# A decoder trunk on one core: other places for the staging of spilled expert activations and for the recurrent layer's modulation rows, and softplus on GpSimd

## The chip, the cores and the metric

The kernel runs on one core of one Trainium2 chip. The metric is the device time of one execution in microseconds. Engines are named as in the profile: PE is TensorE (matmuls), PEld its weight loads, DVE is VectorE, ACT is ScalarE, POOL is GpSimd, SP is SyncE, which here only issues DMA transfers. Each engine has a queue of instructions that it works off in order; an instruction that has to wait holds up all that stand behind it in its queue.

## The reference

The model has two layers. Layer 0 mixes over time with a gated linear recurrence (RG-LRU), layer 1 with multi-head latent attention; in both a PEER layer of 128 x 128 experts follows. Sequence 512, width 1024, all in fp32. Cut to what this change touches:

```python
mod = (silu(c) @ ada_w[l] + ada_b[l])             # six rows of 1024 for each layer
sh1, sc1, g1, sh2, sc2, g2 = split(mod, 6)
h = rmsnorm(x, norm_mix_g[l]) * (1 + sc1) + sh1
gate_in, rec_in = split(h @ w_in, 2)
gate = gelu(gate_in)
xc = causal convolution of rec_in, 4 taps
r, i = sigmoid(xc @ wa + ba), sigmoid(xc @ wx + bx)      # four blocks of 256
log_a = -8 * r * softplus(-lam)
a, b = exp(log_a), sqrt(-expm1(2 * log_a)) * (i * xc)
y = (gate * linear_scan(a, b)) @ w_out
x = x + g1 * y
h = rmsnorm(x, norm_ffn_g[l]) * (1 + sc2) + sh2
x = x + g2 * peer(h)
```

`peer` takes for each token and head the 16 best pairs of two lists of 128 keys, and adds up `g * gelu(h . u[e]) * v[e]` over the experts `e` chosen.

## The kernel before

**Layout and arithmetic.** Activations lie transposed, [128 features, 512 tokens], eight such blocks for the width. A matmul in fp32 is made of three in a shorter format (`mm3`, lines 187 to 189): each operand is split in a high part, a copy on ACT (line 162), and a low part, the difference, mostly on DVE (line 163). A weight tile of 512 KB (128x1024) is loaded by SP into a ring of four buffers `raw`, and split into `whi` and `wlo`, of which there are three each.

**Modulation rows.** `ada(n)` makes 128 of the values of `mod`: SP loads 512 KB (`ada_raw`, line 147), and one DVE instruction multiplies them by silu(c) and sums (line 151) into a column of `mod`. There are 112 of them. `adas(n)` takes the next n from the list `todo`. Layer 0's first norm uses the first 16, the residual of the recurrent layer columns 16 to 23, the norm behind it 24 to 39.

**The recurrent layer.** Norm and the recurrent half of the input projection (`rec`), the convolution (line 385, three DVE steps for each of eight blocks), eight gate blocks (`gate`, line 391, each one weight tile `w_in` and 24 matmuls), the block matrices (`ri`, line 403), the decay (lines 408 to 417), the scan, the product with the gate, its split (`yh`, `yl`), the output projection (`wo`), the residual (line 282) and the sum of squares of the next norm (`nacc`, line 226), which `st` (line 232) sums over the partitions. `softplus_neg` (lines 285 to 328) works on a tile of 128x8 with some fifty short instructions; the decay reads its results `sp_s2` and `sp_s4`. 24 modulation rows are issued in two groups of 12, the first after the convolution's last step, the second after the fourth product with the gate (`held`), through two buffers of the pool `late`.

**PEER.** Three of the four blocks of 128 tokens are done densely: for each of 128 expert groups t, the product with `u` (`u_part`), gelu, multiplication by the routing weights (`weigh`), and the product with `v` (`v_part`), which adds up in PSUM over all t. The fourth block's experts are gathered row by row (`gather_steps`): 256 gathers on GpSimd's queue for each layer, each with one DVE step (lines 1131 and 1136). The routing weights are made in groups and written to DRAM (`wscr`). While that goes on, the products with `u` of the first 93 groups are done already (`LEAD`). Of these, 8 stay in the space of `x`, 9 in a ring of 12 buffers `gact`, and the next 76 (`SPILL`) are written to DRAM (`gscr`) from a staging tile `gsp` with three buffers (lines 908 to 910). `gsp` belongs to the pool `dec`, which closes at line 994. The pool `vp` opens next, and gets the same space: it has `wt` (the routing weights of eight groups, 1.5 MB, line 1007), and the split products `ah` and `al`. `wfirst` (line 1003) has the weights of the first two groups in another pool. In the loop over t, `gact` is loaded back from `gscr` nine groups ahead of its use. The list `wts` shares the gathers that are left over the groups (`goal`).

**What sets the order.** The program is written in a tile framework that orders the instructions of each engine by a simulated time line; `issue_after(i)` keeps an instruction behind another one. Buffers are waited for by semaphores, and a tile in a space that another pool has used waits for all that used it there.

## Time and profile before

| what | value |
|---|---|
| runs | 3152.28, 3153.51, 3155.0 us; median 3153.51 |
| the profiled execution's own time | 3153.72 us |
| its span (the page's first line) | 3151.9 us |
| granted TensorE clock over the span | 0.977 |
| PE, DVE, ACT, POOL busy | 95%, 82%, 44%, 27% |
| DMA | 821 MB, mean 261 GB/s |

The stages follow each other in time: the recurrent layer to about 213 us; layer 0's routing with the products with `u` to 812; its accumulation over the groups to 1515; attention to 1840; layer 1's PEER layer to about 3110, with the start of its accumulation at about 2440. In the rows of the profile a wait stands as "engine tile line <- engine or DMA that ended it: total us, count, longest". In a time line a row has start, length, engine, line, operation, tiles and, in brackets, the idle time before it with what ended it.

### The profile page before, as it was taken

Reading aid. Unit: us, or ns where it says so; the run is one execution under the profiler, and the core shown is the slowest. Engines: PE = TensorE matmul, PEld = TensorE weight load, DVE = VectorE, ACT = ScalarE, POOL = GpSimd, SP = SyncE. Lnnn points to the kernel's source line nnn. Section 1 sums busy time; section 2 is a strip of 40 time slices with the busy share of each in tenths; the row PEclk is TensorE's granted clock in tenths of the full one; section 3 lists DMA queues with packets and bytes.
Section 4 is the critical chain, followed back from the end, with each engine's and each line's share of the span. In section 5 each row is a group of like instructions: output and inputs, shape, how many; then the busy total and the mean of one; then the engine's idle time right before and its main releaser. Section 6 shows DMA issues by size and latency. Waiting matters only on the chain.

```text
span 3151.9 us, 43413 instructions
## 1 busy us (share of the span) xinstructions
PE 2996.1 (95%) x15462; PEld 2651.3 (84%) x15462; DVE 2571.8 (82%) x4895; ACT 1387.8 (44%) x1974; POOL 854.5 (27%) x653
## 2 busy tenths in 40 slices
PE   7989999999899999999899989999999899999997
PEld 6569999999777889998677679999999788889996
DVE  8879999897788878888668768999886777778886
ACT  5643255555233333333466542355554333333333
POOL 0000004342123214444256500014432311134440
PEclk9989999999999999999899999999999999999999
DMA  6644568998989999999213244469998999999994
GB/s 248 202 139 145 175 222 305 313 338 317 325 303 365 347 353 323 336 342 317 71 47 107 76 142 137 138 224 330 321 337 303 353 320 306 322 314 344 338 331 141
DMA packets 345112, 821.15 MB, mean 261 GB/s; under 512 B 33600, under 2 KB 179136, under 8 KB 338496
## 3 DMA queue, kind: packets, MB, share of 16 engines
q1 hardware_dynamic: 239632, 460.91, 43.9%
q0 software_dynamic: 73728, 268.47, 24.2%
q10 hardware_dynamic: 31536, 89.00, 7.4%
q8 instruction: 122, 2.00, 0.3%
q14 instruction: 94, 0.77, 0.1%
HBM read 730.98 MB, written 87.29 MB: 260 GB/s over the span
## 4 chain that ended last, share of the span: by engine, by line
PE 55%; DVE 6%; DMA 2%; ACT 2%; issue 2%; POOL 1%; DVEq 0%; SPq 0%; POOLq 0%; ACTq 0%
PE acc L188 8%; PE acc L187 8%; PE acc L189 8%; PE u L187 7%; PE u L189 7%; PE u L188 7%; PE wps L857 3%; DMA vraw<-in_v_dram 1%; PE pq L187 1%; PE pq L188 1%; PE pq L189 1%; ACT p L667 1%; DVE vl L163 1%; DVE ada_junk L151 1%; DVE p L662 1%
## 5 line engine op out<-in xcount | busy, mean ns | idle before, releaser
L1127 POOL DMA_INDIRECT grow<-in_u_dram,idx x256 | 345.0, 1348 | 1371.2 <-DVE oh L804 706.0
L187 PE MATMUL u<-hh,wlo 128*128 128x384 f32 x2048 | 690.8, 337 | 3.0 <-ACT gsp L909 3.0
L189 PE MATMUL u<-hh,whi 128*128 128x384 f32 x2048 | 688.5, 336 | 0.0
L188 PE MATMUL u<-hl,whi 128*128 128x384 f32 x2048 | 687.1, 335 | 0.0
L187 PE MATMUL acc<-vh,al 128*128 128x512 f32 x1536 | 570.3, 393 | 40.2 <-DVE al L163 30.6
L188 PE MATMUL acc<-vl,ah 128*128 128x512 f32 x1536 | 603.1, 393 | 0.0
L189 PE MATMUL acc<-vh,ah 128*128 128x512 f32 x1536 | 603.0, 393 | 0.0
L1127 POOL DMA_INDIRECT grow<-in_v_dram,idx x256 | 350.1, 1368 | 685.0 <-DVE gacc L1136 383.1
L163 DVE TENSOR_TENSOR wlo<-raw,whi 128x1024 fp32r<-128x1024 f32 x315 | 383.3, 1218 | 113.2 <-ACT whi L162 111.5
L163 DVE TENSOR_TENSOR vl<-vraw,vh 128x1024 fp32r<-128x1024 f32 x256 | 313.2, 1224 | 163.9 <-ACT vh L162 158.9
L162 ACT ACTIVATE whi<-raw 128x1024 fp32r<-128x1024 f32 (+2 forms) x372 | 358.3, 964 | 143.4 <-PE acc L189 30.4
L187 PEld LDWEIGHTS u<-hh,wlo 128*128 128x128 f32 x2048 | 386.5, 189 | 6.5 <-ACT gsp L909 3.7
L188 PEld LDWEIGHTS u<-hl,whi 128*128 128x128 f32 x2048 | 385.9, 188 | 2.7
L189 PEld LDWEIGHTS u<-hh,whi 128*128 128x128 f32 x2048 | 385.7, 188 | 0.0
L187 PEld LDWEIGHTS acc<-vh,al 128*128 128x128 f32 x1536 | 290.8, 190 | 104.2 <-issue 21.1
L189 PEld LDWEIGHTS acc<-vh,ah 128*128 128x128 f32 x1536 | 290.6, 189 | 61.4
L188 PEld LDWEIGHTS acc<-vl,ah 128*128 128x128 f32 x1536 | 291.1, 190 | 59.6 <-DVE vl L163 0.3
L1136 DVE SCALAR_TENSOR_TENSOR gacc<-grow,gdot,gacc 128x1024 f32<-128x1024 f32 x254 | 324.9, 1279 | 17.2 <-DMA grow<-in_v_dram,idx 16.0
L162 ACT ACTIVATE vh<-vraw 128x1024 fp32r<-128x1024 f32 x256 | 268.4, 1050 | 156.4 <-DMA vraw<-in_v_dram 54.1
L162 ACT ACTIVATE ah<-gact 128x384 fp32r<-128x384 f32 x240 | 125.8, 524 | 460.6 <-PE acc L189 257.9
L1131 DVE CUSTOM_DVE_ANT_0 grow<-grow,hn 128x1024 f32<-128x1024 f32 x256 | 309.3, 1219 | 9.2 <-DMA grow<-in_u_dram,idx 8.9
L860 ACT ACTIVATE stg<-wps 128x512 f32<-128x512 f32 x192 | 187.3, 1108 | 54.7 <-PE wps L857 46.2
(345 smaller groups left out, 4193.6 us busy)
## 6 DMA issues: line engine op xcount, KB each, us to landing
raw<-in_uT_dram SPq DMA_DIRECT2D x256, 512.0 KB
vraw<-in_v_dram SPq DMA_DIRECT2D x256, 512.0 KB
ada_raw<-in_adaw_dram SPq DMA_DIRECT2D x112, 512.0 KB
wscr<-stg ACTq DMA_DIRECT2D x48, 1024.0 KB
wt<-wscr SPq DMA_DIRECT2D x32, 1536.0 KB
gscr<-gsp ACTq DMA_DIRECT2D x152, 192.0 KB
gact<-gscr SPq DMA_DIRECT2D x152, 192.0 KB
raw<-in_w_pq_dram SPq DMA_DIRECT2D x32, 512.0 KB
```

The lines of the kernel that those rows point to most:

```text
L151: nc.vector.tensor_tensor_reduce(junk, raw, self.csil, op0=OP.mult, op1=OP.add, scale=1.0, scalar=b, accum_out=col)
L162: nc.scalar.activation(hi, src, AF.Copy)
L163: return (eng or nc.vector).tensor_tensor(lo, src, hi.bitcast(F32), op=OP.subtract)
L187: nc.tensor.matmul(out, al, bh, start=first, stop=False)
L188: nc.tensor.matmul(out, ah, bl, start=False, stop=False)
L189: return nc.tensor.matmul(out, ah, bh, start=False, stop=last)
L662: nc.vector.tensor_tensor_reduce(p, sp, mb[:, b, :], op0=OP.add, op1=OP.max, scale=SCALE, scalar=FMIN, accum_out=st[:, 0, b:b + 1])
L857: last = nc.tensor.matmul(wps[:, t * P:t * P + P], oo[:, n4 + a, :, t], pr[:, q * n4 + a, :, t], start=q == 0, stop=q == 1)
L860: nc.scalar.activation(stg[:, :, c:c + 4].rearrange("p e t -> p t e"), wps.rearrange("p (t e) -> p t e", t=4), AF.Copy, scale=1.0 / GSCALE)
L1127: nc.gpsimd.indirect_dma_start(out=row, out_offset=None, in_=tabs[s], in_offset=bass.IndirectOffsetOnAxis(ap=idx[:, k:k + 1], axis=0))
L1131: nc.vector.tensor_tensor_reduce(row, row, hn, op0=OP.mult, op1=OP.add, scale=1.0, scalar=0.0, accum_out=col)
L1136: nc.vector.scalar_tensor_tensor(acc, row, col, acc, op0=OP.mult, op1=OP.add)
```

## The change

1. **Staging.** `gsp` is allocated in the pool `acts`, where the ring of 12 becomes nine buffers `gact` and three `gsp` (`ring(t)`). The staging uses those three; three of each twelve reloads use them too. `dec` holds no staging any more.
2. **Modulation rows.** Of the 24, 8 come in the pool `early` (7 buffers) behind the last normed block, 6 behind the convolution, and 10 behind the split of the last block of `y` (`lo`).
3. **Softplus.** All its DVE instructions but three (two steps that make `r`, and the reciprocal) go to GpSimd.
4. **Gathers.** In layer 0 the weight of the groups 8 to 83 in `wts` is 0.45 instead of 0.6; the sum of gathers is unchanged.

```diff
@@ Trunk.adas @@
-    def adas(self, n, pool=None, stop=112):
+    def adas(self, n, pool=None, stop=112, bufs=2):
...
-            self.ada(self.todo.pop(0), pool)
+            self.ada(self.todo.pop(0), pool, bufs)
@@ Trunk.normed @@
-        self.nc.vector.tensor_tensor(t, self.x[:, k, :], rs, op=OP.mult)
+        self.last_xn = self.nc.vector.tensor_tensor(t, self.x[:, k, :], rs, op=OP.mult).ins
@@ softplus_neg @@
-        nc.vector.tensor_scalar(n, n, -12582912.0, None, op0=OP.add)
+        nc.gpsimd.tensor_scalar(n, n, -12582912.0, None, op0=OP.add)
         r = t("r")
         nc.vector.scalar_tensor_tensor(r, n, -0.693359375, y, op0=OP.mult, op1=OP.add)
         nc.vector.scalar_tensor_tensor(r, n, 2.12194440e-4, r, op0=OP.mult, op1=OP.add)
...
         for i in range(7, -1, -1):
-            nc.vector.tensor_tensor(p, p, r, op=OP.mult)
-            nc.vector.tensor_scalar(p, p, 1.0 / math.factorial(i), None, op0=OP.add)
+            nc.gpsimd.tensor_tensor(p, p, r, op=OP.mult)
+            nc.gpsimd.tensor_scalar(p, p, 1.0 / math.factorial(i), None, op0=OP.add)
...
         nc.vector.reciprocal(w, w)
-        nc.vector.tensor_tensor(w, w, z, op=OP.mult)
+        nc.gpsimd.tensor_tensor(w, w, z, op=OP.mult)
@@ rglru @@
+                self.todo = [*range(16, 40), *range(96, 112), *range(40, 96)]
+                with tc.issue_after(self.last_xn):
+                    self.adas(8, early, bufs=7)
...
-            self.todo = [*range(16, 40), *range(96, 112), *range(40, 96)]
             with tc.issue_after(conv):
-                self.adas(12, late)
-            with tc.issue_after(held):
-                self.adas(12, late)
+                self.adas(6, late)
+            with tc.issue_after(lo):
+                self.adas(10, late)
@@ peer @@
-            acts = st.enter_context(tc.tile_pool(name=f"acts{l}", bufs=RING))
+            acts = st.enter_context(tc.tile_pool(name=f"acts{l}", bufs=1))
...
+            def ring(t):
+                held = (t - KC) % RING < RING - 3
+                return acts.tile([P, ND], F32, name="gact" if held else "gsp", bufs=RING - 3 if held else 3)
...
-                    g = dpool.tile([P, ND], F32, name="gsp", bufs=3)
+                    g = acts.tile([P, ND], F32, name="gsp", bufs=3)
...
-                    gact[t] = acts.tile([P, ND], F32, name="gact")
+                    gact[t] = ring(t)
...
-            wts = [0.2 if t < KC else 0.6 if t < KC + SPILL else 2.6 if t < tail else 1.0 if t < P - 2 else 0.0 for t in range(P)]
+            wts = [0.2 if t < KC else (0.45, 0.6)[l] if t < KC + SPILL else 2.6 if t < tail else 1.0 if t < P - 2 else 0.0 for t in range(P)]
...
-                        gact[j] = acts.tile([P, ND], F32, name="gact")
+                        gact[j] = ring(j)
```

In the order of instructions, line numbers in the changed program are up to five higher. The first place is SP's queue at the change from routing to accumulation in layer 0 (`vraw` are loads of `v`, `x_69` a reload of the residual). Before:

```order
L1003 DMA wfirst_7900<-wscr_97 128x8x32 [waits DMAHW7_49,DMAHW1_49]
L147 DMA ada_raw_8061<-in_adaw_dram 128x1024 [waits DMAHW3_49,DMAHW2_49,DVE_49]
L1023 DMA vraw_8070<-in_v_dram 128x1024 [waits DMAHW5_49,DVE_49]
L1023 DMA vraw_8099<-in_v_dram 128x1024 [waits DMAHW7_49,DMAHW6_49,DVE_49]
L1023 DMA vraw_8131<-in_v_dram 128x1024 [waits DMAHW3_49,DMAHW1_49,DVE_49]
L147 DMA ada_raw_8155<-in_adaw_dram 128x1024 [waits DMAHW2_49,DMAHW0_49,DVE_49]
L1007 DMA wt_7904<-wscr_97 128x24x128 [waits DMAHW3_49,DMAHW4_49,DMAHW0_49,DMAHW6_49,PE_49,Activation_49]
L1007 DMA wt_8219<-wscr_97 128x24x128 [waits DMAHW5_49]
```

And now:

```order
L1008 DMA wfirst_7900<-wscr_97 128x8x32 [waits DMAHW6_49,DMAHW4_49]
L1012 DMA wt_7904<-wscr_97 128x24x128 [waits DMAHW7_49,PE_49]
L1012 DMA wt_8219<-wscr_97 128x24x128 [waits DMAHW0_49]
L147 DMA ada_raw_8061<-in_adaw_dram 128x1024 [waits DMAHW2_49,DVE_49]
L1028 DMA vraw_8070<-in_v_dram 128x1024 [waits DMAHW4_49,DVE_49]
L1028 DMA vraw_8102<-in_v_dram 128x1024 [waits DMAHW6_49,DMAHW3_49,DVE_49]
```

The two loads of `wt` moved from behind three loads of `v` and two modulation rows to right behind `wfirst`, and the first of them waits for one DMA semaphore and PE in place of four, PE and ACT.

The second place is DVE's queue around the convolution: where the split of the second gate weight stands. Before (`wlo_643` is that split):

```order
L324 TENSOR_TENSOR sp_p_582<-sp_p_582,sp_m_628 128x8
L163 TENSOR_TENSOR wlo_643<-raw_641,whi_642 128x1024
L326 TENSOR_SCALAR sp_s2_631<-sp_p_582 128x8
L327 TENSOR_SCALAR sp_s4_632<-sp_p_582 128x8
L385 SCALAR_TENSOR_TENSOR xc_499<-rec_500,vecs_74,xc_499 128x511
```

And now (`wlo_675` is that split; the convolution's first row stands at the top):

```order
L388 SCALAR_TENSOR_TENSOR xc_531<-rec_532,vecs_74,xc_531 128x511
L151 ISA ada_junk_511,mod_92<-ada_raw_509,csil_66,vecs_74 128x1024
...
L388 SCALAR_TENSOR_TENSOR xc_541<-rec_542,vecs_74,xc_541 128x511
L151 ISA ada_junk_515,mod_92<-ada_raw_513,csil_66,vecs_74 128x1024
...
L388 SCALAR_TENSOR_TENSOR xc_591<-rec_592,vecs_74,xc_591 128x511
L388 SCALAR_TENSOR_TENSOR xc_541<-rec_542,vecs_74,xc_541 128x509
L163 TENSOR_TENSOR wlo_675<-raw_673,whi_674 128x1024
```

The split moved from ahead of the convolution to behind 13 of its 24 steps and two modulation rows; the short softplus rows are gone from DVE.

The third place is DVE's queue behind the split of the last block of `y`. Before (`raw_1579` is the first weight of the next layer):

```order
L163 TENSOR_TENSOR yl_1160<-tanh_1082,yh_1159 128x512
L163 TENSOR_TENSOR wlo_1455<-raw_1453,whi_1454 128x1024
L163 TENSOR_TENSOR wlo_1581<-raw_1579,whi_1580 128x1024
L282 SCALAR_TENSOR_TENSOR x_69<-wo_1259,mod_92,x_69 128x512
```

And now:

```order
L163 TENSOR_TENSOR yl_1192<-tanh_1114,yh_1191 128x512
L151 ISA ada_junk_1221,mod_92<-ada_raw_1219,csil_66,vecs_74 128x1024
...
L151 ISA ada_junk_1225,mod_92<-ada_raw_1223,csil_66,vecs_74 128x1024
...
L163 TENSOR_TENSOR wlo_1449<-raw_1447,whi_1448 128x1024
L151 ISA ada_junk_1229,mod_92<-ada_raw_1227,csil_66,vecs_74 128x1024
...
L163 TENSOR_TENSOR wlo_1581<-raw_1579,whi_1580 128x1024
L151 ISA ada_junk_1245,mod_92<-ada_raw_1243,csil_66,vecs_74 128x1024
...
L282 SCALAR_TENSOR_TENSOR x_69<-wo_1259,mod_92,x_69 128x512
```

Ten modulation rows came in behind that split, seven of them ahead of the first residual step and three among the others.

More of the change, by code (lines that the diff above doesn't have):

```diff
@@ L294, in softplus_neg @@
         nc.scalar.activation(y, lam, AF.Abs)
-        nc.vector.tensor_scalar(y, y, -1.0, -87.0, op0=OP.mult, op1=OP.max)
+        nc.gpsimd.tensor_scalar(y, y, -1.0, -87.0, op0=OP.mult, op1=OP.max)
         n = t("n")
-        nc.vector.tensor_scalar(n, y, 1.0 / math.log(2.0), 12582912.0, op0=OP.mult, op1=OP.add)
-        nc.vector.tensor_scalar(n, n, -12582912.0, None, op0=OP.add)
+        nc.gpsimd.tensor_scalar(n, y, 1.0 / math.log(2.0), 12582912.0, op0=OP.mult, op1=OP.add)
+        nc.gpsimd.tensor_scalar(n, n, -12582912.0, None, op0=OP.add)
         r = t("r")
@@ L302, in softplus_neg @@
         p = t("p")
-        nc.vector.memset(p, 1.0 / math.factorial(8))
+        nc.gpsimd.memset(p, 1.0 / math.factorial(8))
         for i in range(7, -1, -1):
-            nc.vector.tensor_tensor(p, p, r, op=OP.mult)
-            nc.vector.tensor_scalar(p, p, 1.0 / math.factorial(i), None, op0=OP.add)
+            nc.gpsimd.tensor_tensor(p, p, r, op=OP.mult)
+            nc.gpsimd.tensor_scalar(p, p, 1.0 / math.factorial(i), None, op0=OP.add)
         ni = t("ni", I32)
-        nc.vector.tensor_scalar(ni, n, 127.0, 8388608.0, op0=OP.add, op1=OP.mult)
+        nc.gpsimd.tensor_scalar(ni, n, 127.0, 8388608.0, op0=OP.add, op1=OP.mult)
         z = t("z")
-        nc.vector.tensor_tensor(z, p, ni.bitcast(F32), op=OP.mult)
+        nc.gpsimd.tensor_tensor(z, p, ni.bitcast(F32), op=OP.mult)
         w = t("w")
-        nc.vector.tensor_scalar(w, z, 2.0, None, op0=OP.add)
+        nc.gpsimd.tensor_scalar(w, z, 2.0, None, op0=OP.add)
         nc.vector.reciprocal(w, w)
-        nc.vector.tensor_tensor(w, w, z, op=OP.mult)
+        nc.gpsimd.tensor_tensor(w, w, z, op=OP.mult)
         w2 = t("w2")
-        nc.vector.tensor_tensor(w2, w, w, op=OP.mult)
-        nc.vector.memset(p, 2.0 / 17)
+        nc.gpsimd.tensor_tensor(w2, w, w, op=OP.mult)
+        nc.gpsimd.memset(p, 2.0 / 17)
         for i in (15, 13, 11, 9, 7, 5, 3, 1):
-            nc.vector.tensor_tensor(p, p, w2, op=OP.mult)
-            nc.vector.tensor_scalar(p, p, 2.0 / i, None, op0=OP.add)
-        nc.vector.tensor_tensor(p, p, w, op=OP.mult)
+            nc.gpsimd.tensor_tensor(p, p, w2, op=OP.mult)
+            nc.gpsimd.tensor_scalar(p, p, 2.0 / i, None, op0=OP.add)
+        nc.gpsimd.tensor_tensor(p, p, w, op=OP.mult)
         m = t("m")
-        nc.vector.tensor_scalar(m, lam, -1.0, 0.0, op0=OP.mult, op1=OP.max)
-        nc.vector.tensor_tensor(p, p, m, op=OP.add)
+        nc.gpsimd.tensor_scalar(m, lam, -1.0, 0.0, op0=OP.mult, op1=OP.max)
+        nc.gpsimd.tensor_tensor(p, p, m, op=OP.add)
         s2, s4 = t("s2"), t("s4")
-        nc.vector.tensor_scalar(s2, p, -2.0, None, op0=OP.mult)
-        nc.vector.tensor_scalar(s4, p, -4.0, None, op0=OP.mult)
+        nc.gpsimd.tensor_scalar(s2, p, -2.0, None, op0=OP.mult)
+        nc.gpsimd.tensor_scalar(s4, p, -4.0, None, op0=OP.mult)
         return s2, s4
@@ L441, in rglru @@
                         last_gelu = nc.scalar.activation(gg[j], gg[j], AF.Gelu).ins
-                    dv = nc.vector.tensor_tensor(tt[j], tt[j], gg[j], op=OP.mult).ins
-                    if j == 3:
-                        held = dv
+                    nc.vector.tensor_tensor(tt[j], tt[j], gg[j], op=OP.mult)
                     ys.append(self.pair(pool, "y"))
-                    self.split(ys[j][0], ys[j][1], tt[j])
-            self.todo = [*range(16, 40), *range(96, 112), *range(40, 96)]
+                    lo = self.split(ys[j][0], ys[j][1], tt[j]).ins
             with tc.issue_after(conv):
-                self.adas(12, late)
-            with tc.issue_after(held):
-                self.adas(12, late)
+                self.adas(6, late)
+            with tc.issue_after(lo):
+                self.adas(10, late)
             outs = [self.bank("wo") for _ in range(KC)]
```

## The prediction

> **What bounds the kernel now.** I read the page first, then busy time by stage, then TensorE's waits in the stages that the change touches. The first line is the span, the second the shares of it; the table has, for each stretch in us, its length and the busy time (with instructions) of PE, PEld, DVE, ACT and POOL, then the granted clock, the DMA share and GB/s.
>
> ```profile
> span 3151.9 us, 43413 instructions
> PE 2996.1 (95%) x15462; PEld 2651.3 (84%) x15462; DVE 2571.8 (82%) x4895; ACT 1387.8 (44%) x1974; POOL 854.5 (27%) x653
> ...
> 100.00:200.00 100.00, 85.20 (x304) 60.99 (x303) 85.64 (x128) 52.15 (x75) 0.00 (x0) 0.88 0.54 178
> 120.00:140.00 20.00, 13.46 (x32) 6.86 (x31) 20.00 (x29) 10.63 (x17) 0.00 (x0) 0.74 0.46 148
> 300.00:400.00 100.00, 100.00 (x542) 92.42 (x541) 94.43 (x442) 29.18 (x39) 0.00 (x0) 1.00 0.51 163
> 823.40:837.20 13.80, 11.17 (x37) 8.68 (x37) 8.74 (x11) 2.49 (x4) 2.88 (x2) 0.78 1.07 333
> 837.20:1000.00 162.80, 152.80 (x650) 124.89 (x651) 136.91 (x212) 57.45 (x77) 40.08 (x27) 0.97 0.96 335
> 1000.00:1200.00 200.00, 196.55 (x866) 161.37 (x865) 158.44 (x220) 72.40 (x96) 47.71 (x36) 1.00 0.98 340
> 1475.00:1515.00 40.00, 40.00 (x183) 33.80 (x182) 31.52 (x37) 16.61 (x22) 3.91 (x4) 1.00 0.74 240
> 2463.70:2500.00 36.30, 36.23 (x153) 29.82 (x154) 28.55 (x35) 11.38 (x16) 12.02 (x9) 0.95 1.05 376
> ```
>
> TensorE is 95% busy, so an edit is worth what it gives back of TensorE's idle and slow time. The recurrent layer (row 100 to 200) has much of both: 14.8 us idle, and 85.2 us busy at a clock of 0.88, or 85.2 × 0.12 = 10 us lost, while DVE is full in the row from 120. From 300 to 400 TensorE has no gap, so what the recurrent layer gains is carried to the end. From 823 to 1200 TensorE waits for 16 us, but there the DMA engines stand at 0.96 to 1.07: two limits lie close together. At 1475 to 1515 TensorE is the limit alone.
>
> **The modulation rows.** DVE's group of the 24 reductions, TensorE's longest waits from 66 to 212 us (total, count, longest), and pieces of the time line (start, length):
>
> ```profile
> L151 DVE CUSTOM_DVE_ANT_0 ada_junk<-ada_raw,csil,vecs 128x1024 bf16<-128x1024 f32 x24 | 30.7, 1280 | 7.1 <-DMA ada_raw<-in_adaw_dram 7.0
> ...
> PE wo L187 <- ACT yh L162: 8.3, 1, 8.3
> PE ri L403 <- ACT gate L393: 3.3, 1, 3.3
> PE gate L187 <- ACT g L405: 3.2, 1, 3.2
> ...
> 66.32 12.12 DVE L385 SCALAR_TENSOR_TENSOR xc<-rec,vecs,xc 128x511 f32<-128x511 f32 x18 [1.09 <-ACT xc L377]
> 85.90 0.33 SPq L147 DMA_DIRECT2D ada_raw<-in_adaw_dram  x1
> 89.51 1.28 DVE L151 CUSTOM_DVE_ANT_0 ada_junk<-ada_raw,csil,vecs 128x1024 bf16<-128x1024 f32 x1 [1.29 <-DMA ada_raw<-in_adaw_dram]
> 79.63 0.50 PE L187 MATMUL gate<-hmh,wlo 128*128 128x512 f32 x1 [0.59 <-DVE wlo L163]
> 186.87 0.69 DVE L163 TENSOR_TENSOR yl<-tanh,yh 128x512 fp32r<-128x512 f32 x1 [0.70 <-ACT yh L162]
> 210.02 0.69 DVE L226 TENSOR_TENSOR nacc<-nacc,sq 128x512 f32<-128x512 f32 x1
> ```
>
> All 24 stand in DVE's full stretch, ahead of the scan, whose end starts the output projection (the 8.3 us wait for `yh`). After the change 6 stay, 2 of the early 8 fall in it, and 16 leave it: 16 × 1.28 = 20.5 us, and up to 7.0 us of waits for transfers. TensorE can get back no more than the waits ahead of the projection and the slow clock: 8.3 + 3.3 + 3.2 + 10 = 25 us. I take 22, since about this much leaves DVE. Two things are given back. First, the split of the second gate weight stood ahead of the convolution; now 13 convolution steps and two reductions come first: 13 × 12.12/18 + 2 × 1.28 = 11.3 us from 66.3, and with the split itself, taken like a reduction of the same tile, it ends near 78.9. The third gate began at 79.6 after a wait of 0.6; the second is 24 matmuls earlier, which at full clock (196.55 / 866 = 0.227 us each in the row from 1000) are 5.4 us, at 73.6: 5 us late. Second, ten reductions now stand behind the last `yl`, where the way to the last sum of squares took 210.71 - 187.56 = 23.2 us. DVE is not full there, but 12.8 us more have to fit in, and two buffers with a landing 3.6 us after the issue (85.90 to 89.51) feed them: nothing to 10 us, I take 5. Sum: 22 - 5 - 5 = **-12**, with ends at +6 (the projection's start moves by only 9) and -20.
>
> **Softplus on GpSimd.** The trace has no 128x8 operation there. DVE's group of one of the steps, GpSimd's smallest and nearest groups (busy, mean ns), and the first reader of the result:
>
> ```profile
> L320 DVE TENSOR_SCALAR sp_p<-sp_p 128x8 f32<-128x8 f32 x8 | 1.4, 171 | 0.2
> ...
> L163 POOL TENSOR_TENSOR wlo<-raw,whi 128x256 fp32r<-128x256 f32 x40 | 32.9, 829 | 55.9 <-ACT whi L162 55.5
> L1230 POOL MEMSET const-float32-1.0<- 128x1 f32 x1 | 0.1, 107 | 0.0
> ...
> 93.61 0.81 ACT L410 ACTIVATE tanh<-g,sp_s 128x512 f32<-128x512 f32 x1
> ```
>
> So one costs 0.107 to 0.829 us. 18 of them stand between the two steps left on DVE and DVE's reciprocal, which sits ahead of the splits of the weights: 1.9 to 15 us. Beside them DVE has two reductions, two weight splits and four 128x512 steps like `yl`: 4 × 1.28 + 4 × 0.69 = 7.9 us. 128x8 is nearer the memset in size, so I take 0.3, or 5.4 us: covered, **0**; at 0.829, or without this cover, +7 to +15 for DVE, of which TensorE's queue ahead passes on half, so +8. All 47 end, at 0.829 each, 39 us after the start near 30, ahead of 93.6. DVE gives up 47 × 0.171 = 8.0 us there, which hides the six early reductions that come before 66 us, 6 × 1.28 = 7.7.
>
> One page speaks against this edit: the Trainium skill, GPSIMD Engine Reference, "8. Key points", has GpSimd share its SBUF interfaces with VectorE, in contention with DVE instructions of two SBUF inputs. By it the additions beside it would take longer. The trace agrees in sign for a split-like addition beside GpSimd work and one without:
>
> ```profile
> 1565.09 1.76 DVE L226 TENSOR_TENSOR nacc<-nacc,sq 128x512 f32<-128x512 f32 x1
> 1580.64 0.69 DVE L226 TENSOR_TENSOR nacc<-nacc,sq 128x512 f32<-128x512 f32 x1 [0.76 <-ACT sq L225]
> ```
>
> By that rule the edit would come out some us dearer, inside the +8.
>
> **Spill staging, layer 0.** From the last `u` matmul to the accumulation of the third expert block:
>
> ```profile
> 812.06 0.34 PE L189 MATMUL u<-hh,whi 128*128 128x384 f32 x1
> 823.47 0.76 PE L187 MATMUL acc<-vh,al 128*128 128x512 f32 x1 [11.07 <-DVE al L163]
> 837.20 0.50 PE L187 MATMUL acc<-vh,al 128*128 128x512 f32 x1 [2.56 <-DVE al L163]
> 821.45 0.94 ACT L162 ACTIVATE ah<-x 128x384 fp32r<-128x384 f32 x2 [7.57 <-DMA gscr<-gsp]
> 796.74 0.49 SPq L1003 DMA_DIRECT2D wfirst<-wscr  x1
> 821.45 7.26 SPq L1007 DMA_DIRECT2D wt<-wscr  x2
> ```
>
> `ah` and `wt` lie in the space of the pool that holds the staging, so both start at 821.45, when the last spill has landed. With the staging elsewhere `ah` waits for its product, and `wt` is issued behind `wfirst`, at about 797. The gap of 812.4 to 837.2 holds 36 matmuls of 0.227, 8.2 us; 24.8 - 8.2 = 16.6 us can go. From 837 to 1200 another 10.0 + 3.5 us of idle and 152.8 × 0.03 = 4.6 of slow clock can, if data come: TensorE's bound is 35. The data bound it lower: 13.8 × 333 + 162.8 × 335 + 200 × 340 = 127.1 MB from 823 to 1200, which at 340 GB/s take 373.9 us of 376.6, so 2.7 us, and at 376 (the row from 2463.7) 38.6. The lighter weight takes gather steps out of these blocks; the order has 7 fewer by block 85. A gather's transfer and its DVE step:
>
> ```profile
> q0 software_dynamic: 73728, 268.47, 24.2%
> ...
> L1136 DVE SCALAR_TENSOR_TENSOR gacc<-grow,gdot,gacc 128x1024 f32<-128x1024 f32 x254 | 324.9, 1279 | 17.2 <-DMA grow<-in_v_dram,idx 16.0
> ```
>
> 512 gathers move 268.47 MB, 0.524 each: 7 × 0.524 / 0.340 = 10.8 us. The DMA limit is then 2.7 + 10.8 = 13.5, and I take 14, since the gap itself was at 1.07. At the end the last nine blocks take 16 instead of 10: 6 × 1.28 = 7.7 us of DVE, where it had 8.5 us idle of 40: 2 us back. **-12**, ends 0 and -28.
>
> The Trainium skill, DMA: Bandwidth & Descriptors, "Where 436 GB/s comes from", gives about 358 GB/s of HBM for a core. By it the 127.1 MB take 355 us, and the stage would gain nearer 30 than 14; the long rows stay under it, at 335 and 340, the short one passes it.
>
> **Spill staging, layer 1.** The same place, with the chain of waits:
>
> ```profile
> 2439.89 1.06 ACT L162 ACTIVATE vh<-vraw 128x1024 fp32r<-128x1024 f32 x1 [3.65 <-PE u L189]
> 2442.12 1.02 DVE L1012 TENSOR_TENSOR x<-x,wfirst 128x384 f32<-128x384 f32 x2
> 2449.10 0.77 PE L187 MATMUL acc<-vh,al 128*128 128x512 f32 x1 [9.24 <-DVE al L163]
> 2463.76 0.50 PE L187 MATMUL acc<-vh,al 128*128 128x512 f32 x1 [3.88 <-DVE al L163]
> ...
> 2441.36 4.42 DMA gscr<-gsp
> 2445.91 14.62 DMA wt<-wscr
> ```
>
> Here the split of `v` and the products still stand behind the last `u`: 2442.12 + 0.51 and two splits of half a us, 2443.6, instead of 2449.1. 5.5 us go, then the 3.88 of the second gap with the 2.8 of slow clock before it: 12.2, less 2 for a DMA share of 1.05 behind it: **-10**, ends -4 and -18.
>
> **The sum.** -12 + 0 - 12 - 10 = -34. The profiled execution took 3153.7 us, 0.2 over the median, so about **3120 us**.
>
> **The rivals.** *The DMA engines stay the limit*: `wt` comes early, but what follows comes no earlier, since shares were 0.96 and more. 3 and 4 at the transitions and 8 in the recurrent layer: 3139. For it the shares, against it the fewer gathers. *All of it comes back*: 20 + 28 + 15 = 63, 3091; for it 376 GB/s in one row, against it 340 in the long ones. *The change doesn't do what it says in one place*: another tile of the released space still holds `wt`, only the recurrent layer's 12 are left: 3140; against it the wait lists in the order. *Slower*: each late reduction waits for its own transfer in DVE's queue, and the residuals and splits behind it wait too. If the two buffers don't overlap, ten cost 10 × (landing + 1.28), where the sum has 23.2 + 5; the 34 gained are used up at 62.2 us, a landing of 4.9. At 6 it is 72.8 - 28.2 - 34 = +11: 3164. Against it is the landing of 3.6 us; for it the transfers of the next weights beside them.
>
> **The numbers.** Forecast 0.50, DMA limit 0.20, all 0.17, wrong place 0.06, slower 0.07. Within 0.2% (6.3 us) is what a measurement here can't tell from no change. Of the second and fourth case a fifth ends there, 0.05; faster 0.88, slower 0.07. The range goes from all (3090) to short of no change (3148).
>
> **What would show it.** Right: `wt` issued behind `wfirst` and no `ah` waiting for a spill; TensorE's gap at layer 0's transition under 5 us and at layer 1's near 4; `wo` waiting less than 8.3 us and `st` near 200 instead of 210.9. Wrong: the reciprocal on DVE waiting for GpSimd; reductions behind the last `yl` waiting for their transfers; 837 to 1200 as long as before at a DMA share of 1.0.

## The result, and the profile after

The change took 3117.0 us (median of four runs, 3115.5 to 3120.0) against 3153.3 before: ratio 0.9887, 95% interval 0.9873 to 0.9902, so 36 us or 1.1% faster. The forecast was 3120. The profiled execution of the change took 3117.2 us. Its page:

```profile
span 3115.4 us, 43400 instructions
PE 2987.1 (96%) x15462; PEld 2648.1 (85%) x15462; DVE 2565.5 (82%) x4848; ACT 1385.4 (44%) x1974; POOL 900.8 (29%) x700
```

TensorE did the same 15462 matmuls in 9 us less of busy time (2996.1 before, at a mean granted clock of 0.977, now 0.980), and the rest of the 36.5 us of span is idle time that went. Where it went is told by the time line, by the start of the same matmul in both (`pq` are the first products of a PEER layer, in its routing stage, `u` the products with `u`, `acc` those of the accumulation; times in us):

| matmul | before | after | lead | gained in the stage |
|---|---|---|---|---|
| first `pq` of layer 0 (recurrent layer done) | 215.4 | 211.1 | 4.4 | 4.4 |
| last `u` ahead of layer 0's accumulation | 812.1 | 806.6 | 5.4 | 1.1 |
| first `acc` of layer 0 | 823.5 | 807.0 | 16.5 | 11.1 |
| last `acc` of layer 0 | 1520.7 | 1496.1 | 24.7 | 8.2 |
| first `pq` of layer 1 (attention done) | 1844.5 | 1820.1 | 24.3 | -0.3 |
| last `u` ahead of layer 1's accumulation | 2439.5 | 2415.3 | 24.2 | -0.1 |
| first `acc` of layer 1 | 2449.1 | 2419.7 | 29.4 | 5.2 |
| last `acc` of layer 1 | 3128.2 | 3092.0 | 36.2 | 6.8 |

Here a lead, once made, is held to within a microsecond or so through what TensorE bounds (the routing stages and attention). By the steps of the prediction: the recurrent layer with softplus gave 4.4 us (forecast 12), layer 0's transition and accumulation 19.3 (forecast 12), layer 1's 12.0 (forecast 10).

**The recurrent layer.** TensorE's waits from 17 to 215 us, and rows of its and DVE's time line:

```profile
PE st L232 <- DVE nacc L226: 14.3, 1, 14.3
PE gate L187 <- DVE wlo L163: 4.0, 1, 4.0
...
68.95 0.39 PE L187 MATMUL gate<-hmh,wlo 128*128 128x512 f32 x1
78.60 0.79 PE L187 MATMUL gate<-hmh,wlo 128*128 128x512 f32 x1 [4.05 <-DVE wlo L163]
...
169.51 0.69 DVE L163 TENSOR_TENSOR yl<-tanh,yh 128x512 fp32r<-128x512 f32 x1
...
171.44 1.66 SPq L147 DMA_DIRECT2D ada_raw<-in_adaw_dram  x2
...
176.41 1.28 DVE L151 CUSTOM_DVE_ANT_0 ada_junk<-ada_raw,csil,vecs 128x1024 bf16<-128x1024 f32 x1 [2.53 <-DMA ada_raw<-in_adaw_dram]
179.28 1.28 DVE L151 CUSTOM_DVE_ANT_0 ada_junk<-ada_raw,csil,vecs 128x1024 bf16<-128x1024 f32 x1 [1.58 <-DMA ada_raw<-in_adaw_dram]
202.73 3.07 DVE L226 TENSOR_TENSOR nacc<-nacc,sq 128x512 f32<-128x512 f32 x4
```

The waits of 8.3 us for `yh`, 3.3 for the gate and 3.2 for `g` are gone, and the last `yl` comes 17.4 us earlier (169.5, before 186.9). Most of that is given back behind it: from the end of the last `yl` to the end of the last sum of squares (called the tail below) it takes 205.80 - 170.20 = 35.6 us, before 23.2, and `st` waits 14.3 us instead of 4.4. Five of the ten late reductions wait for their transfer, 2.53 us the longest, 7.0 in all; the one reduced at 176.41 was issued at 171.44, 5 us before. The tail before and now, in the columns of the prediction's table of stretches:

```profile
187.56:210.71 23.15, 18.88 (x83) 15.23 (x82) 14.78 (x19) 8.97 (x12) 0.00 (x0) 1.00 0.46 166
```

```profile
170.20:205.80 35.60, 20.89 (x91) 16.63 (x89) 28.19 (x42) 8.84 (x12) 0.00 (x0) 0.83 0.73 236
```

DVE's 28.19 us of work and the 7.0 of waits make up the whole of it but 0.4: with the ten rows there DVE bounds the tail, which it did not before (14.78 of 23.15). The second gate starts at 78.60 behind a wait of 4.05, as the order had shown (its split was forecast to end near 78.9).

**GpSimd.** Softplus in the time line, of DVE (three rows) and of GpSimd:

```profile
24.84 1.27 DVE L151 CUSTOM_DVE_ANT_0 ada_junk<-ada_raw,csil,vecs 128x1024 bf16<-128x1024 f32 x1
...
26.12 1.21 DVE L163 TENSOR_TENSOR wlo<-raw,whi 128x1024 fp32r<-128x1024 f32 x1
30.48 0.20 DVE L313 RECIPROCAL sp_w<-sp_w 128x8 f32<-128x8 f32 x1 [3.14 <-POOL sp_p L317]
...
25.09 1.08 POOL L305 TENSOR_TENSOR sp_p<-sp_p,sp_r 128x8 f32<-128x8 f32 x1
26.26 1.16 POOL L306 TENSOR_SCALAR sp_p<-sp_p 128x8 f32<-128x8 f32 x1
27.51 0.20 POOL L305 TENSOR_TENSOR sp_p<-sp_p,sp_r 128x8 f32<-128x8 f32 x1
27.80 0.23 POOL L306 TENSOR_SCALAR sp_p<-sp_p 128x8 f32<-128x8 f32 x1
28.11 0.20 POOL L305 TENSOR_TENSOR sp_p<-sp_p,sp_r 128x8 f32<-128x8 f32 x1
28.40 0.23 POOL L306 TENSOR_SCALAR sp_p<-sp_p 128x8 f32<-128x8 f32 x1
...
32.63 0.53 POOL L319 TENSOR_TENSOR sp_p<-sp_p,sp_w 128x8 f32<-128x8 f32 x1
33.24 1.22 POOL L320 TENSOR_SCALAR sp_p<-sp_p 128x8 f32<-128x8 f32 x1
```

One operation takes 0.20 or 0.23 us while DVE stands still, from 27.3 to 30.5, and 0.34 to 1.25 us while DVE works. The chain of two engines slows itself: GpSimd is held up by DVE until DVE has to wait for GpSimd, 3.14 us. The Trainium skill, SBUF — State Buffer, "SBUF: two separate sides", says that the port pair which the two share is locked for a whole instruction and the loser blocks; the trace agrees, since a GpSimd step that starts near the start of a DVE split or reduction lasts about as long as that instruction (1.08 to 1.22 against 1.21 and 1.27 us): those at 25.09 and 26.26 end 0.06 and 0.09 us behind the DVE rows beside them.

**The transitions.** SP's queue and TensorE in layer 0, then TensorE in layer 1:

```profile
791.31 0.56 SPq L1008 DMA_DIRECT2D wfirst<-wscr  x1
791.97 6.99 SPq L1012 DMA_DIRECT2D wt<-wscr  x2
...
806.64 0.34 PE L189 MATMUL u<-hh,whi 128*128 128x384 f32 x1
806.97 0.47 PE L187 MATMUL acc<-vh,al 128*128 128x512 f32 x1
...
2419.70 0.77 PE L187 MATMUL acc<-vh,al 128*128 128x512 f32 x1 [4.07 <-issue]
```

`wt` is issued right behind `wfirst`, 29 us before it was (791.97 after 821.45). In layer 0 the accumulation follows the last `u` without a gap (0.33 us from start to start, before 11.41); in layer 1 the gap falls to 4.1 us, as forecast.

### The profile page after: what moved, and what is told of

The parts are those of the page before. It is cut to its first block, busy times and chain, and to the rows that moved or that the text cites. A ratio compares the mean times of both kernels' runs of the same rounds, so it can differ in the third digit from the quotient of the medians.

```text
span 3115.4 us, 43400 instructions
## 1 busy us (share of the span) xinstructions
PE 2987.1 (96%) x15462; PEld 2648.1 (85%) x15462; DVE 2565.5 (82%) x4848; ACT 1385.4 (44%) x1974; POOL 900.8 (29%) x700
## 3 DMA queue, kind: packets, MB, share of 16 engines
q0 software_dynamic: 73728, 268.47, 24.3%
## 5 line engine op out<-in xcount | busy, mean ns | idle before, releaser
L1132 POOL DMA_INDIRECT grow<-in_v_dram,idx x256 | 366.4, 1431 | 681.1 <-DVE gacc L1141 389.4
L187 PE MATMUL acc<-vh,al 128*128 128x512 f32 x1536 | 544.9, 392 | 14.6 <-ACT vh L162 10.5
L162 ACT ACTIVATE ah<-gact 128x384 fp32r<-128x384 f32 x180 | 94.2, 523 | 332.2 <-PE acc L189 186.7
L860 ACT ACTIVATE stg<-wps 128x512 f32<-128x512 f32 x192 | 186.9, 1106 | 54.5 <-PE wps L857 40.8
```

What stands on the lines that cost most here:

```text
L162: nc.scalar.activation(hi, src, AF.Copy)
L187: nc.tensor.matmul(out, al, bh, start=first, stop=False)
L860: nc.scalar.activation(stg[:, :, c:c + 4].rearrange("p e t -> p t e"), wps.rearrange("p (t e) -> p t e", t=4), AF.Copy, scale=1.0 / GSCALE)
L1132: nc.gpsimd.indirect_dma_start(out=row, out_offset=None, in_=tabs[s], in_offset=bass.IndirectOffsetOnAxis(ap=idx[:, k:k + 1], axis=0))
```

## The experiments

Each ratio is to the kernel before, run on the same chip in the same session, where its median was 3153.1 to 3155.7 us; medians of different rows are from different sessions, so the ratios are what compares. The marks by stage come from the one profiled execution of each; they resolve about a microsecond in the recurrent layer (first `pq` of kernels with the same order there: 211.1, 210.7 and 209.8), where the interval of a time is 7 to 20 us wide. Elsewhere they are coarser: attention, which no run changed, took 321.7 to 327.6 us, and layer 0's way from the last `u` to the last `acc` took 687.0 to 691.7 in the six kernels with the change's staging and weight and the gap of 0.3 (the change, 4, 5, 9, 10, 11) and 708.7 and 710.9 in two with those of before. Layer 1 repeats within about 1 us (1283.1 to 1284.1 without the new staging, 1271.6 to 1272.1 with it, run 10 apart). The gap is from the start of the last `u` matmul to that of the first `acc`; all columns are in us.

| kernel | median us | ratio (95% interval) | span | first `pq` | gap at layer 0 | layer 0, last `u` to last `acc` | layer 1, first `pq` to last `acc` |
|---|---|---|---|---|---|---|---|
| before | 3153.3 | | 3151.9 | 215.4 | 11.4 | 708.7 | 1283.7 |
| the change | 3117.0 | 0.9887 (0.9873, 0.9902) | 3115.4 | 211.1 | 0.3 | 689.4 | 1271.9 |
| 1 rows and softplus alone | 3149.2 | 0.9979 (0.9967, 0.9991) | 3147.9 | 210.7 | 11.1 | 710.9 | 1284.1 |
| 2 staging alone | 3139.9 | 0.9949 (0.9932, 0.9967) | 3133.3 | 215.6 | 3.3 | 699.9 | 1271.8 |
| 3 lighter weight alone | 3149.7 | 0.9979 (0.9969, 0.9990) | 3148.7 | 214.6 | 11.6 | 703.5 | 1283.1 |
| 4 the change, softplus on DVE | 3114.0 | 0.9869 (0.9848, 0.9890) | 3110.8 | 205.6 | 0.3 | 690.5 | 1271.9 |
| 5 the change, no late rows | 3121.0 | 0.9894 (0.9872, 0.9916) | 3118.0 | 214.0 | 0.3 | 689.4 | 1272.0 |
| 6 the change, three buffers | 3117.7 | 0.9886 (0.9864, 0.9908) | 3112.8 | 205.6 | 4.1 | 693.4 | 1271.6 |
| 7 the change, late reciprocal | 3118.7 | 0.9885 (0.9865, 0.9906) | 3117.6 | 207.4 | 3.2 | 689.6 | 1271.9 |
| 8 softplus on DVE, ten and six | 3120.6 | 0.9896 (0.9875, 0.9918) | 3115.2 | 206.7 | 4.1 | 694.6 | 1271.8 |
| 9 softplus on DVE, three buffers | 3110.1 | 0.9862 (0.9831, 0.9894) | 3107.1 | 203.6 | 0.3 | 687.0 | 1272.1 |
| 10 as 9, `ah` first | 3111.7 | 0.9865 (0.9834, 0.9897) | 3107.7 | 203.0 | 0.3 | 691.7 | 1269.3 |
| 11 as 10, lighter weight in layer 1 | 3113.3 | 0.9868 (0.9838, 0.9899) | 3111.7 | 203.5 | 0.3 | 690.7 | 1271.7 |
| 12 the change, weight 0.6 | 3124.1 | 0.9900 (0.9876, 0.9923) | 3119.5 | 209.8 | 0.3 | 695.3 | 1272.0 |

### 1 The modulation rows and softplus alone

Against the change, this kernel has `gsp` in the pool `dec` and the one weight for both layers, as before:

```diff
-                    g = acts.tile([P, ND], F32, name="gsp", bufs=3)
+                    g = dpool.tile([P, ND], F32, name="gsp", bufs=3)
...
-            wts = [0.2 if t < KC else (0.45, 0.6)[l] if t < KC + SPILL else ...
+            wts = [0.2 if t < KC else 0.6 if t < KC + SPILL else ...
```

> The kernel before with the modulation rows and softplus of the change, and nothing else. First theory (the parts add up, and what the recurrent layer gains is carried to the end because TensorE bounds what follows): the first pq matmul at 211.1 us instead of 215.4, the last u matmul about 5.4 earlier, the first acc still behind the wait of 11 us for the last spill, in all 4 to 5.5 us faster (ratio 0.9983 to 0.9987). Rival (accumulation of layer 0 is bound by the DMA engines, which give the lead back): pq earlier just so, but the end of layer 0's accumulation not earlier, 0 to 1 us in all.

First `pq` at 210.65, 4.8 us earlier; layer 0's accumulation ends 3.7 us earlier and the span is 4.0 shorter. So the lead of the recurrent layer is carried to the end, except for about a microsecond: the first theory. By the spans these two parts together are worth 4 of the 36 us; the interval of the times, 3 to 10 us, allows for that.

### 2 The staging alone

```diff
-                    g = dpool.tile([P, ND], F32, name="gsp", bufs=3)
+                    g = acts.tile([P, ND], F32, name="gsp", bufs=3)
```

(with the function `ring`, and its two uses for `gact[t]` and `gact[j]`.)

> The kernel before with the staging in the acts ring, and nothing else. First theory (both transitions waited for the last spill, and TensorE has room behind them): the gap ahead of the first acc of layer 0 goes from 11.1 to under 1 us, in layer 1 from 9.2 to about 4, and layer 0's accumulation ends 15 to 19 us earlier than before, layer 1's 10 to 13: 25 to 32 us in all. Rival (the DMA engines are the limit from 823 to 1200, so only fewer gathers give the lead its worth): layer 0 keeps 3 us at its end, layer 1 10: 13 us.

The wait for the last spill is gone in both layers. TensorE's first `acc` of layer 0 in this run:

```profile
815.88 0.76 PE L187 MATMUL acc<-vh,al 128*128 128x512 f32 x1 [2.92 <-issue]
```

Layer 1 gained 11.9 us (1283.7 to 1271.8), all that it gained in the change. Layer 0 gained 8.8, between the two expectations: neither the full 15 to 19, nor the 3 that the DMA engines were thought to leave. The whole fell between them too: 16 us by the medians, where they said 25 to 32 and 13. Its first `acc` still stands 3.3 us behind the last `u`, which the change has not; run 10 says why.

### 3 The lighter weight alone

```diff
-            wts = [0.2 if t < KC else 0.6 if t < KC + SPILL else ...
+            wts = [0.2 if t < KC else (0.45, 0.6)[l] if t < KC + SPILL else ...
```

> The kernel before with the lighter weight for the gathers in layer 0, and nothing else. First theory (the transition waits for the spill, whatever the gathers do, and TensorE waits little for transfers after 1000 us): the gap of 11.1 us stays, the accumulation is 0 to 4 us shorter. Rival (the DMA engines are the limit there): 7 gathers of 0.524 MB at 340 GB/s less by block 85, layer 0's accumulation 8 to 11 us shorter.

The gap stays (11.2 us idle), and the way to the last `acc` is 5.2 us shorter than before (7.4 shorter than in run 1, which has the same staging and weight as before): between both again. At 5.2, seven gathers less give about half of what their bytes take at 340 GB/s (10.8). The gain is complete by the start of block 72, at about 1137 us, and stays the same to the last block, so the gathers that are put off to the end cost TensorE nothing.

### 4 Softplus back on DVE

```diff
-        nc.gpsimd.tensor_scalar(y, y, -1.0, -87.0, op0=OP.mult, op1=OP.max)
+        nc.vector.tensor_scalar(y, y, -1.0, -87.0, op0=OP.mult, op1=OP.max)
```

(and the same for every other line of the function.)

> The change with softplus back on DVE. First theory (the 3.1 us that DVE waits at the reciprocal and the slower start of the gates are the price, and the 8 us of DVE that GpSimd takes over are worth more, because DVE is full from 60 to 80): the first gate matmul starts as late as in the change or later, the second gate's split later than 77.3, the first pq matmul 2 to 6 us later than 211.1. Rival (the stall outweighs it): the first gate at 68.0 instead of 68.95, pq 1 us earlier.

The first theory fell. TensorE's gates in this run:

```profile
67.05 0.39 PE L187 MATMUL gate<-hmh,wlo 128*128 128x512 f32 x1
79.71 0.50 PE L187 MATMUL gate<-hmh,wlo 128*128 128x512 f32 x1 [1.61 <-DVE wlo L163]
```

The first gate starts at 67.05 instead of 68.95, the wait ahead of a later one is 1.6 us instead of 4.05, and `pq` starts at 205.64 instead of 211.09: the rival's direction, but five times its size. The steps that came back last 0.16 us each on DVE (two groups of eight from the polynomial: 162 and 159 ns), but the next instruction starts 0.07 to 0.09 us behind each, so that the 47 make DVE's busy time 4.2 us longer (2569.7 after 2565.5), and DVE has room for them. So GpSimd's part of the change cost 5.5 us, and the modulation rows alone gave 215.4 - 205.6 = 9.8. Of the 5.5, 2.9 are made by the start of the last `yl` (166.65, in the change 169.51); the other 2.6 are the tail (33.0 us after 35.6), where the reductions wait 4.7 us for their transfers instead of 7.0. Why they wait less there stays open. Over the whole program the two kernels' intervals overlap; the spans differ by 4.6 us.

### 5 No rows behind the last yl

```diff
-                self.adas(6, late)
-            with tc.issue_after(lo):
-                self.adas(10, late)
+                self.adas(16, late)
```

> The change with no modulation row behind the last yl: its ten come with the six behind the convolution. First theory (in the tail a row costs more than its 1.28 us, since it also waits for its transfer; in front of the scan it costs 1.28 less the idle time of DVE): the last yl 10 to 13 us later than 169.5, the way from it to the last sum of squares back at 23 us from 35.9, the first pq matmul within 3 us of 211.1. Rival (DVE is no limit any more between 100 and 160 us, where it had 2 to 5 us idle in each 20): the last yl 4 to 8 us later, pq at 203 to 206.

The first theory held, with the last `yl` later than it said: it ends at 185.3 instead of 170.2, 15 us later for ten rows (forecast 10 to 13), the tail is back at 23.7 us, and `pq` comes at 214.0, 2.9 us later than in the change. A row costs about 1.5 us in front of the scan and 1.2 behind it; moving rows behind the scan is worth little as long as they wait for transfers there.

### 6 Three buffers for the late rows

```diff
-                self.adas(6, late)
+                self.adas(6, late, bufs=3)
             with tc.issue_after(lo):
-                self.adas(10, late)
+                self.adas(10, late, bufs=3)
```

> The change with three buffers instead of two for the rows that come late. First theory (the round trip of a buffer, issue to landing to reduction, sets the pace of the ten): most of the 7 us that DVE waited for those transfers go, st 5 to 7 us earlier than 205.95, pq at 204 to 206. Rival (the DMA engines share their rate between these rows and the weights, so a third buffer makes each landing longer): st 0 to 2 us earlier.

DVE's waits for the rows' transfers from 60 to 215 us (total, count, longest), in the change and in this run:

```profile
DVE ada_junk L151 <- DMA ada_raw<-in_adaw_dram: 10.8, 8, 2.5
```

```profile
DVE ada_junk L151 <- DMA ada_raw<-in_adaw_dram: 3.1, 4, 1.1
```

7.7 us of waiting went and `pq` comes at 205.6, 5.5 us earlier: the round trip of a buffer, from the issue over the landing to the reduction, had set the pace. In this run the transfers issued behind the last `yl` land 4.4 to 6.5 us after their issue. Of the 5.5 us, 4.2 are the tail (31.4 us after 35.6); the last `yl` is 1.3 us earlier too, but so it is in run 12, with two buffers. The whole did not get measurably faster by it (3117.7): of the lead, 1.5 us were gone by the last `u`, and 4 more between it and the last `acc`, where the gap is 4.1 us here.

### 7 The reciprocal held back

```diff
-        nc.vector.reciprocal(w, w)
+        with self.tc.issue_after(self.last_xn):
+            nc.vector.reciprocal(w, w)
```

> The change with softplus on GpSimd, but DVE's reciprocal held behind the last normed block, so that DVE doesn't wait 3.1 us for GpSimd at 27 us. First theory (that wait is the price of GpSimd): DVE has no idle time there, the first gate at about 67 as with softplus on DVE, pq at about 206. Rival (the price comes from the order that the scheduler makes with these rows on GpSimd, with the second gate's split behind 13 convolution steps): gate earlier, but the wait of 4 us ahead of the second gate grows, pq at 209 to 211.

```profile
67.40 0.39 PE L187 MATMUL gate<-hmh,wlo 128*128 128x512 f32 x1
76.89 0.79 PE L187 MATMUL gate<-hmh,wlo 128*128 128x512 f32 x1 [3.89 <-DVE wlo L163]
```

Without the wait of 3.1 us the first gate starts at 67.40, and `pq` at 207.4: 3.7 of the 5.5 us came back with it. The wait ahead of the second gate stays at 3.9 us, as the rival said; it comes with the order, in which the second gate's split stands behind 13 steps of the convolution. But it doesn't delay the scan. The last `yl`, in run 4 and in this one:

```profile
166.65 0.69 DVE L163 TENSOR_TENSOR yl<-tanh,yh 128x512 fp32r<-128x512 f32 x1 [0.70 <-ACT yh L162]
```

```profile
166.45 0.68 DVE L163 TENSOR_TENSOR yl<-tanh,yh 128x512 fp32r<-128x512 f32 x1
```

Up to there the wait at the reciprocal was the whole price of GpSimd. The 1.8 us that are left are in the tail: 34.9 us, with 6.4 of waits for transfers, where run 4 has 33.0 and 4.7.

### 8 Ten rows early, six late

Softplus on DVE as in run 4, three buffers as in run 6, and

```diff
-                self.adas(6, late)
+                self.adas(10, late, bufs=3)
             with tc.issue_after(lo):
-                self.adas(10, late)
+                self.adas(6, late, bufs=3)
```

> Softplus on DVE as before, the rest of the change, but ten rows behind the convolution and six behind the last yl, through three buffers. If the late rows' transfers and GpSimd's price are what the change lost: pq at 201 to 204 instead of 211.1, and the whole 7 to 10 us faster than the change, 3107 to 3110 (ratio about 0.986 to the kernel before). Rival (the rows in front of the scan cost as much as they save behind it): pq at 205 to 207, 3113.

`pq` at 206.7: the rival. Four rows moved in front of the scan cost more than they saved behind it: against run 9, with six and ten, the last `yl` starts 9.1 us later and the tail is 6.1 shorter, and `pq` there is at 203.6. Layer 0's gap of 4.1 us came back. With a median of 3120.6 the kernel missed both forecasts, 3107 to 3110 and the rival's 3113.

### 9 Softplus on DVE, three buffers

Runs 4 and 6 together; six rows behind the convolution, ten behind the last `yl`.

> The change with softplus on DVE and three buffers for the late rows; six rows stay behind the convolution, ten behind the last yl. In its order the first ah of layer 0 stands ahead of the split of the third block of v, as in the change. If the prices of GpSimd (5.5 us at pq) and of the round trip (5.5 us) add up and the order decides the transition: pq at 199 to 202, the gap ahead of layer 0's first acc at 0.3, the whole 9 to 12 us faster than the change, 3105 to 3108 (ratio 0.985). Rival (the gap comes from how early TensorE reaches it, since transfers can't follow): gap 3 to 4 us, 3109 to 3112.

`pq` at 203.6 (forecast 199 to 202), 7.5 us ahead of the change, where the two edits alone gave 5.5 each: they overlap by 3.5. Both take from the same waits, those of the late reductions in the tail: 7.0 us in the change, 4.7 in run 4, 2.9 in run 6, 2.2 here. The gap is 0.3 us, as its order had said. The kernel took 3110.1 us (forecast 3105 to 3108), ratio 0.9862; its span is 8.3 us shorter than the change's. It is the fastest of all here, though its interval (0.9831 to 0.9894) doesn't part it from the change's.

### 10 The first ah ahead of the third split of v

```diff
-                    self.split(ah, al, aw)
+                    hi = nc.scalar.activation(ah, aw, AF.Copy).ins
+                    nc.vector.tensor_tensor(al, aw, ah.bitcast(F32), op=OP.subtract)
+                if t == 1:
+                    grp["ah1"] = hi
...
-                vls.append(self.split(vh, vl, raw).ins)
+                with tc.issue_after(grp["ah1"]) if t == 2 else ExitStack():
+                    vls.append(self.split(vh, vl, raw).ins)
```

> As the one with softplus on DVE and three buffers, and with the split of the third block of v held behind the first two ah, in both layers. If the 4.1 us that layer 1 still waits are the queue on ACT (the first ah behind a split that waits for the last u matmul to free its weight buffer): layer 1's gap falls to 0.3 to 1 us, 3 to 4 us faster in all, 3102 to 3104. Rival (wt or the product on DVE comes no earlier): the gap stays at 3 us or more, 0 to 1 us.

ACT's time line at layer 1's transition, of run 9 (with two rows of DVE) and then of this one, with TensorE's first `acc` of this one:

```profile
2407.39 1.06 ACT L162 ACTIVATE vh<-vraw 128x1024 fp32r<-128x1024 f32 x1 [3.65 <-PE u L189]
2408.48 1.22 DVE L163 TENSOR_TENSOR vl<-vraw,vh 128x1024 fp32r<-128x1024 f32 x1 [2.47 <-ACT vh L162]
2409.62 1.02 DVE L1017 TENSOR_TENSOR x<-x,wfirst 128x384 f32<-128x384 f32 x2
2410.20 0.99 ACT L162 ACTIVATE ah<-x 128x384 fp32r<-128x384 f32 x2 [1.76 <-DVE x L1017]
```

```profile
2411.58 0.99 ACT L1023 ACTIVATE ah<-x 128x384 fp32r<-128x384 f32 x2 [2.53 <-DVE x L1017]
2412.48 1.04 ACT L162 ACTIVATE vh<-vraw 128x1024 fp32r<-128x1024 f32 x1
...
2412.79 0.47 PE L187 MATMUL acc<-vh,al 128*128 128x512 f32 x1 [1.05 <-issue]
```

In run 9 the first `ah` stands behind a split of `v` that waits for a `u` matmul, here the last: on ACT behind its `vh`, and the product `x` that it reads stands on DVE behind its `vl`. With `ah` and its product ahead of that split, TensorE's wait falls from 4.1 to 1.05 us, and layer 1 takes 2.8 us less. So what was left of the gap was the order of the split and the first product in the two queues. The same order goes with the gap at layer 0 in the other runs: where `ah` stands ahead of the third `vh` (the change, 4, 5, 9 to 12) the gap is 0.3, else (2, 6, 7, 8) 3.2 to 4.1. What such a gap costs at layer 0 is not shown: run 7 has one of 3.2 us, and its way to the last `acc` is the change's (689.6 and 689.4), while runs 6 and 8, with 4.1, take 4 to 5 us more. The whole did not get faster than run 9 (3111.7 us, forecast 3102 to 3104), since layer 0's accumulation took 4.7 us more (691.7 after 687.0): it was 1.0 ahead up to about 905 us and lost 5.7 in four steps by 1000, with next to the same order there. What makes that stage vary by so much stays open.

### 11 The lighter weight in layer 1 too

```diff
-            wts = [0.2 if t < KC else (0.45, 0.6)[l] if t < KC + SPILL else ...
+            wts = [0.2 if t < KC else 0.45 if t < KC + SPILL else ...
```

> The same, and the lighter weight for the gathers in layer 1 too. Layer 1's TensorE had nearly no wait behind the transition in the change (its lead of 38 us stays the same from the tenth block to the last), so there is nothing for fewer gathers to give: 0 to 1 us, or 1 to 2 us slower by the gathers that come at the end. Rival (the transfers limit layer 1 just behind the transition too): 2 to 5 us faster.

Layer 1 took 1271.7 us after 1269.3, 2.4 slower: nothing to gain. The gathers that are put off did not cost at the end, as the first theory had allowed for: 0.7 us of the 2.4 were lost ahead of the first `acc`, 1.8 in the 35 us behind it, and nothing from there to the last. The times (3113.3 and 3111.7) don't part the two.

### 12 The change with the weight of before

```diff
-            wts = [0.2 if t < KC else (0.45, 0.6)[l] if t < KC + SPILL else ...
+            wts = [0.2 if t < KC else 0.6 if t < KC + SPILL else ...
```

> The change with the gathers' weight of before (0.6) in layer 0. The way from the last u matmul ahead of the accumulation to its last matmul is 708.7 us before, 703.5 with the lighter weight alone, 699.9 with the staging alone, 689.4 in the change. First theory (the parts add up, and what the change has beyond their sum is the order around the first ah, worth 3 us): 692 to 696. Rival (fewer gathers are worth more once the transition is short, since the transfers are then the limit): 697 to 701, 8 to 11 us slower than the change in this stage.

Layer 0's way is 695.3 us: the first theory. So the staging with the order of the change is worth 708.7 - 695.3 = 13.4 us in layer 0, and the lighter weight 5.9 on top, about what it gave alone (5.2). Against the six kernels with the lighter weight, 687.0 to 691.7, it is 3.6 to 8.3, so the size is known to a few us only; as in run 3 it is complete by block 72 and stays to the last. Run 2 takes 4.6 us more than this run, but run 7 doesn't let that be put down to the order around the first `ah`. The times of this kernel and of the change, ratios 0.9900 and 0.9887, don't part the two. The DMA engines were no harder limit for the short transition. From about the start of the accumulation to 1190 us, this run's row (length, busy time of PE, PEld, DVE, ACT and POOL, clock, DMA share, GB/s):

```profile
805.00:1190.00 385.00, 368.81 (x1607) 301.61 (x1606) 321.69 (x462) 138.78 (x185) 107.63 (x73) 0.99 1.00 349
```

and the change's:

```profile
806.60:1190.00 383.40, 372.85 (x1629) 307.81 (x1628) 316.49 (x455) 139.58 (x187) 95.35 (x67) 0.98 0.98 341
```

## Why the prediction was right, point by point

The total came within 3 us of 3120, but two of its terms, the recurrent layer and layer 0, were off by 7 to 8 us each, in opposite directions. What bounds the kernel and which waits go was right; that the sum fits so closely is luck. Of the signs that the prediction named, `st` near 200 did not come (205.95), and two of the three signs of being wrong did: the reciprocal waits for GpSimd, and the late reductions wait for their transfers.

- **What bounds the kernel.** Right: what a stage gave back of TensorE's idle time was carried to the end (run 1, and the table of leads).
- **Rows out of DVE's full stretch.** Right in the mechanism. I took 22 us for the projection's start; with softplus on DVE (run 4) the last `yl` starts at 166.7, 20 us earlier, and in the change 17.4.
- **The second gate's split.** Right in place and time: at 78.60 after a wait of 4.05, forecast 78.9 and 5. Wrong as a term: run 7 keeps that wait (3.9) and has its last `yl` at 166.45, as early as run 4, so the 5 us taken off for it were not lost at the scan. That 22 - 5 = 17 is next to the 17.4 of the change is luck: the 3 us by which the change falls short of run 4 are GpSimd's.
- **Ten reductions behind the last yl.** The mechanism was right, the size off: 5 us taken, bounds nothing to 10, measured 12.4 in the change. The 23.2 + 5 = 28.2 us of the sum are just what DVE worked in the tail (28.19); the mis-sized part is the 7.0 us of waits on top. I had held the round trip of the two buffers for mostly hidden by a landing of 3.6 us; here it took 5 us from the issue to the reduction (171.44 to 176.41), and a third buffer took 4.2 us of the tail away (run 6). This is the slower rival's mechanism, short of its threshold.
- **Softplus on GpSimd.** Forecast 0, with +8 where the cover is gone; measured +5.5 (run 4). The step that failed is the price of one operation, 0.3 us: the lowest were 0.20, but beside DVE's instructions they were 0.34 to 1.16, so that 18 of them took 10 us instead of 5.4 and DVE waited 3.1. "Some us dearer, inside the +8" was the better forecast, though the other way round: it had DVE's additions take longer, and here GpSimd's steps did. The 8.0 us that DVE was to give up were 4.2 (run 4), since its short instructions overlap.
- **Layer 0's transition.** Right that the gap goes and `wt` follows `wfirst`. Mis-sized: of 13.5 us for the DMA limit I had 2.7 for the staging and 10.8 for the seven gathers. They were 13.4 (run 12) and 5.9, the latter known to a few us only. The 2 us that the last blocks were to give back did not show (runs 3 and 12). The limit of 340 GB/s, taken from the longest row, was not one: over the same stretch the engines moved 349 GB/s at a share of 1.00 in run 12. So the stage's 19.3 us lay between the two limits of the prediction, 13.5 and 35; the rival by which the DMA engines stay the limit fell.
- **Layer 1's transition.** Right: a gap of 4.1 us (forecast near 4), 11.8 us in all for 10.
- **The wrong place.** No other tile held `wt` or `ah` back; that rival fell with the first rows of the transition.
- **The working.** Four small figures don't come out as written. The traces show 8 gathers fewer by block 85, not 7 (147 started, before 155). The 2.8 us of slow clock ahead of layer 1's second gap come out at 2.6 (10.79 us busy for 36 matmuls of 0.227). The rival by which all comes back takes 15 us for layer 1, where the range says 18. The one with the wrong place comes to 3142 with the 12 us that it keeps, not 3140. None of them moves the forecast by more than a microsecond or two.

## What to carry to other kernels

Before a pool closes and another opens in its space, ask which transfer still reads the old one: here the staging of the last spill held back 3 MB of loads and the first operands of the next stage while TensorE waited 11.1 and 9.2 us, and the cure was to allocate it with a ring that lives longer, which left 0 and 4.1. Reductions fed by a transfer each need buffers for the whole round trip, or they wait where they stand; and work moved to GpSimd is priced by what DVE does beside it, not by its size. When a gap falls only in part, look for the instruction that waits in front of the wanted one in the same queue, and see whether the time of the stage falls with the gap.

## What was not expected of the hardware

A GpSimd operation on 128x8 takes 0.20 to 0.23 us beside an idle DVE and up to 1.25 beside a busy one (`sp_p`, line 324, at 49.25), while the DVE instructions beside it keep their length (splits of 128x1024 at 1.21 to 1.23 us with and without). With these short operations the price of sharing thus fell on GpSimd alone, and came to DVE only through the wait at the reciprocal. With long ones on GpSimd it can be otherwise: the prediction's sum of squares of 1.76 us instead of 0.69 starts at 1565.09, beside a GpSimd operation of 1.61 us that had started at 1564.69.

The 16 DMA engines moved 349 GB/s over 385 us of accumulation (run 12), where the longest rows of before had 335 to 340 at shares of 0.96 to 0.98: a share just below 1 was not yet the limit.
